# A gated ConvFFN's down projection as seven block products: TensorE work against GpSimd work

## The chip, the core and the metric

The kernel runs on one core of one Trainium2 chip. The metric is the device time of one execution in microseconds (us). Engines are named as in the profile: PE is TensorE, DVE is VectorE, ACT is ScalarE, POOL is GpSimd, SP is SyncE, which only issues transfers here.

## The reference, cut to what matters

The reference is a decoder block: a token mixer, cross-attention to a memory, and a gated feed-forward part (FFN), each followed by a layer norm. Only the FFN and the last norm are touched. `x` is 1024 tokens by 1024 features, `D_FF` is 2816, all float32:

```
u = jnp.einsum('bsd,df->bsf', x, w_up)                  # 1024 -> 2*2816
u = conv_general_dilated(u, conv_w, width 3, causal, per channel) + conv_b
a, g = jnp.split(u, 2, axis=-1)
ff = jnp.einsum('bsf,fd->bsd', silu(g) * a, w_down)     # 2816 -> 1024
x = layer_norm(ALPHA * x + ff, ln3_g, ln3_b)
```

## The kernel before

Every float32 product is made of three passes on TensorE: each operand is split into a rounded high part (a cast on ACT) and the remainder, the low part (one subtraction, on DVE or POOL), and high x high, high x low and low x high are accumulated. So each operand costs one cast and one subtraction each time that it is split.

The FFN has two stages. The **up stage** (`begin`, `end`, `product`) goes through 22 chunks `f` of 128 gated features. Its product is already made in 2x2 blocks by seven block products per chunk (factors A11, A12, S3, S1, S2, A22, S4 of the weight; B11, B21, T3, T1, T2, T4, B22 of the activation); a product is 12 matmuls. For a chunk POOL makes seven low parts and two block sums (`sw`, L1022), DVE makes the other two sums, the convolution (L1098, L1099) and the gating (L1121), and the gated rows of the chunk, `za`, go to a buffer in device memory, `hid`, by a transfer on SP (L1123).

The **down stage** (`load_step`, `fill`, `part`) accumulates over the 22 chunks twice, once for each half of the 1024 output columns. A step is one chunk of one half: the weight rows `w_down` (128x512) and the gated rows `hid` (128x1024) come in, both are cast on ACT, the low part of the weight (`wd`) is made on POOL and that of the rows (`hl`) on DVE, and TensorE runs 8 row tiles x 3 matmuls of 512 columns into 8 PSUM banks. `fill` loads up to `DAHEAD` steps ahead, through three `raw` buffers and through slots of one pool of 47 equal buffers (`Slots`), which are given out in the order in which they were put back. In the last `DROWS` chunks the loop runs row tile by row tile; after each tile DVE adds it to the scaled residual `y`, and in the second half the layer norm of that tile follows: statistics on DVE, two very small operations on POOL (L784, L785), a scaling on ACT and an addition on POOL (L794).

The order of instructions on each engine isn't that of the code: a scheduler orders them by a timeline of its own before the kernel runs, and each engine then takes its queue strictly in that order. A slot's new user waits for its last one.

## Time and profile before

| | |
|---|---|
| median of three runs | 1621.48 us (1620.51 to 1630.96) |
| profiled execution, its own time | 1628.77 us |
| its span, first to last instruction | 1627.1 us |
| mean granted TensorE clock | 0.989 |
| down stage on TensorE, first to last matmul | 1372.94 to 1619.46 us |
| busy in the span: PE / DVE / ACT / POOL | 97% / 60% / 44% / 42% |

Each row of the profile gives a group of instructions or one of them; "idle before" is the time its engine stood still ahead of it, and the arrow names what ended that. Matmuls overlap, so the time that one takes in a stream is read from the starts of neighbours, not from its own duration.

### The profile page before, as it was taken

The numbers are of one execution on the slowest core, as the hardware profiler recorded it, in microseconds if no ns is written. First come the engines' busy times: TensorE is split into PE (matmuls) and PEld (weight loads), VectorE is DVE, ScalarE is ACT, GpSimd is POOL, SyncE is SP. The second block draws the span as 40 slices with busy tenths as digits, with TensorE's granted clock in tenths as the row PEclk, the third lists the DMA queues.
The fourth block names the chain that finished last, engine by engine and source line by source line (L and its number), as shares of the span: only waits on it lengthen the run. The fifth ranks groups of instructions, "written<-read, shape, count | busy, mean of one in ns | idle before, by whom it ended". The sixth has DMA issues, their size and how long they took to land.

```text
span 1627.1 us, 21298 instructions
## 1 busy us (share of the span) xinstructions
PE 1579.6 (97%) x8084; PEld 1336.9 (82%) x8084; DVE 972.0 (60%) x1524; ACT 718.8 (44%) x1235; POOL 688.4 (42%) x540
## 2 busy tenths in 40 slices
PE   8999998999998999999999999999999999999997
PEld 6788887988887988888988878788888888778886
DVE  3856967367577756642456567777666667333325
ACT  4726564156566761133442144454444544442411
POOL 5302222144344741111102657877777773332316
PEclk9999999799999999999999999999999999999999
DMA  6301112132231592311382222222222226663622
GB/s 182 79 1 27 53 52 59 33 91 58 72 107 44 158 281 87 130 40 39 106 264 100 78 65 65 91 78 78 91 81 92 87 71 221 210 203 113 208 61 104
DMA packets 153365, 165.11 MB, mean 101 GB/s; under 512 B 6352, under 2 KB 121112, under 8 KB 153264
## 3 DMA queue, kind: packets, MB, share of 16 engines
q1 hardware_dynamic: 149776, 152.07, 30.4%
q10 hardware_dynamic: 3168, 11.54, 1.9%
q8 instruction: 63, 1.03, 0.3%
q14 instruction: 38, 0.31, 0.1%
q0 software_dynamic: 320, 0.16, 0.0%
HBM read 127.01 MB, written 32.54 MB: 98 GB/s over the span
## 4 chain that ended last, share of the span: by engine, by line
PE 77%; DVE 8%; DMA 6%; ACT 4%; POOL 3%; issue 2%; SPq 0%; POOLq 0%; DVEq 0%; ACTq 0%
PE ps_pj L174 20%; PE ps_S L174 17%; PE ps_t L1078 12%; PE ps_S L1078 6%; PE ps_t L174 5%; PE ps_t L1193 4%; PE ps_S L1193 4%; PE ps_pj L1078 3%; PE ps_pj L1193 2%; DMA raw<-hid 2%; POOL wop L1045 1%; PE ps_t L650 1%; DMA raw<-in_ffn_w_down_dram 1%; PE ps_t L213 1%; DVE p L632 1%
## 5 line engine op out<-in xcount | busy, mean ns | idle before, releaser
L174 PE MATMUL ps_pj<-xT,wh 128*128 128x512 f32 x976 | 313.4, 397 | 0.9 <-DVE KL L593 0.9
L185 POOL TENSOR_TENSOR wl<-raw,wh 128x1024 fp32r<-128x1024 f32 x48 | 120.5, 2511 | 223.5 <-ACT wh L183 213.5
L174 PEld LDWEIGHTS ps_pj<-xT,wh 128*128 128x128 f32 x976 | 180.4, 189 | 34.9 <-DVE KL L593 1.4
L1078 PE MATMUL ps_t<-T,wop 128*128 128x512 f32 x792 | 191.8, 393 | 2.7 <-ACT yg L1107 2.1
L174 PE MATMUL ps_pj<-xT,wl 128*128 128x512 f32 x488 | 192.6, 395 | 0.0
L1078 PEld LDWEIGHTS ps_t<-T,wop 128*128 128x128 f32 x792 | 149.3, 189 | 35.0 <-ACT yg L1107 2.5
L1045 POOL TENSOR_TENSOR wop<-raw,wop 128x512 fp32r<-128x512 f32 x66 | 110.8, 1690 | 86.8 <-ACT wop L1044 86.7
L1045 POOL TENSOR_TENSOR wop<-sw,wop 128x512 fp32r<-128x512 f32 x88 | 134.7, 1553 | 21.8 <-ACT wop L1044 21.8
L1171 POOL TENSOR_TENSOR wd<-raw,wd 128x512 fp32r<-128x512 f32 x44 | 61.0, 1387 | 139.4 <-ACT wd L1170 136.4
L185 DVE TENSOR_TENSOR hl<-raw,hh 128x1024 fp32r<-128x1024 f32 x44 | 54.6, 1242 | 106.1 <-ACT hh L183 106.1
L174 PEld LDWEIGHTS ps_pj<-xT,wl 128*128 128x128 f32 x488 | 91.8, 188 | 17.6
L174 PE MATMUL ps_S<-wh,mh 128*128 128x512 f32 x256 | 100.1, 391 | 0.7 <-ACT mh L183 0.7
L174 PE MATMUL ps_S<-wh,ml 128*128 128x512 f32 x256 | 100.2, 392 | 0.0
L174 PE MATMUL ps_S<-wl,mh 128*128 128x512 f32 x256 | 99.9, 390 | 0.0
L784 POOL TENSOR_SCALAR mv<-mv 128x1 f32<-128x1 f32 x24 | 28.8, 1198 | 159.4 <-DVE mv L783 159.4
L183 ACT CAST wh<-raw 128x1024 fp32r<-128x1024 f32 x64 | 67.2, 1049 | 59.8 <-issue 23.1
L1044 ACT CAST wop<-sw 128x512 fp32r<-128x512 f32 x88 | 54.6, 622 | 86.9 <-POOL sw L1022 58.1
L183 ACT CAST hh<-raw 128x1024 fp32r<-128x1024 f32 x44 | 46.2, 1050 | 90.3 <-DMA raw<-hid 53.7
L1193 PE MATMUL ps_S<-wd,hh 128*128 128x512 f32 x264 | 81.5, 393 | 1.7 <-ACT hh L183 1.7
L1193 PE MATMUL ps_t<-wd,hh 128*128 128x512 f32 x264 | 80.6, 389 | 0.0
L1022 POOL TENSOR_TENSOR sw<-raw 128x512 f32<-128x512 f32 x42 | 66.5, 1582 | 14.6 <-PE ps_t L1078 9.6
L627 POOL TENSOR_TENSOR cdg<-cbc,tri 128x128 f32<-128x128 f32 x64 | 33.0, 518 | 82.0 <-DVE mx L632 61.5
(295 smaller groups left out, 3677.0 us busy)
## 6 DMA issues: line engine op xcount, KB each, us to landing
raw<-in_ffn_w_up_dram SPq DMA_DIRECT2D x44, 512.0 KB, 3.8
raw<-hid SPq DMA_DIRECT2D x44, 512.0 KB, 4.0
raw<-in_w_in_dram SPq DMA_DIRECT2D x24, 512.0 KB, 4.0
hid<-z SPq DMA_DIRECT2D x22, 512.0 KB, 2.6
raw<-in_ffn_w_down_dram SPq DMA_DIRECT2D x44, 256.0 KB, 2.9
raw<-in_xa_wkv_dram SPq DMA_DIRECT2D x16, 512.0 KB, 4.4
x_dram<-y ACTq DMA_DIRECT2D x16, 512.0 KB, 2.6
y<-x_dram SPq DMA_DIRECT2D x16, 512.0 KB, 4.6
```

Source lines behind the costliest of these rows:

```text
L174: nc.tensor.matmul(o, l, r, start=start, stop=stop)
L183: nc.scalar.copy(h, src)
L185: eng.tensor_tensor(l, src, h.bitcast(F32), ALU.subtract)
L213: nc.tensor.transpose(ps[:, k * P:(k + 1) * P], nat[:, kk * P:(kk + 1) * P], ident)
L627: nc.gpsimd.tensor_tensor(cdg, cbc[:, dg], tri, ALU.add)
L784: nc.gpsimd.tensor_scalar(mv[:, 2:3], mv[:, 1:2], LN_EPS, None, ALU.add)
L1022: eng.tensor_tensor(sums[pair][:, i], x0, x1, op)
L1044: nc.scalar.copy(w[:, 0], src)
L1045: nc.gpsimd.tensor_tensor(w[:, 1], src, w[:, 0].bitcast(F32), ALU.subtract)
L1078: nc.tensor.matmul(ps, w[:, part, ws], r, start=first and k == 0 and i == 0, stop=k == 3 and i == 2, skip_group_check=not first)
L1171: nc.gpsimd.tensor_tensor(w[:, 1], raw, w[:, 0].bitcast(F32), ALU.subtract)
L1193: nc.tensor.matmul(banks[st][:, lo:hi], a[:, ss], w[:, r, lo:hi], start=f == 0 and i == 0, stop=f == NF - 1 and i == 2, skip_group_check=l ...
```

## The change

The down projection too is made in 2x2 blocks by seven block products. The blocks are: 512 tokens by 512 tokens, 11 chunks of features by 11 chunks, 512 output columns by 512. For that the chunks are taken in pairs `i` and `11 + i`, also in the up stage. The gated rows are stored as the seven left factors: A11, A12, A22 as they are, S3 = h0 left half minus h0 right half, S1, S2 and S4 as sums and differences of the two chunks of a pair; three of these four are made on POOL and one on DVE at the end of a pair. The seven right factors come from whole rows of `w_down`, which now stay in slots (`wr`); T3, T2 and T4 are made from them by subtractions on POOL, partly in place. A step is one pair `i` of one product `q`: one left factor (128x512) comes in, both factors are cast and split as before, and TensorE runs 4 row tiles x 3 matmuls. `plan` sets the order of the products; each accumulates into one of two groups of four banks, which are added into `y` at the end of each product. Four row tiles are complete after the fifth product and normalized there, the others at the end. `DAHEAD` is 7 and `DROWS` is 7.

```
+    chunks = [c for i in range(HC) for c in (i, HC + i)]
...
+        if f < HC:
+            nc.sync.dma_start(hid_dram[f]["A11"][:, 0], za[:, hs(0)])
+            held[f] = za
+            return
+        to, h0, h1 = hid_dram[f - HC], held.pop(f - HC), za
+        s31, s24 = get([P, 2, 512], name="s31"), get([P, 2, 512], name="s24")
+        nc.sync.dma_start(to["A12A22"], h1.rearrange("p (j s) -> p j s", j=2))
+        nc.gpsimd.tensor_tensor(s31[:, 0], h0[:, hs(0)], h0[:, hs(1)], ALU.subtract)
+        nc.vector.tensor_tensor(s31[:, 1], h0[:, hs(1)], h1[:, hs(1)], ALU.add)
+        nc.sync.dma_start(to["S3S1"], s31)
+        nc.gpsimd.tensor_tensor(s24[:, 0], s31[:, 1], h0[:, hs(0)], ALU.subtract)
+        nc.gpsimd.tensor_tensor(s24[:, 1], h1[:, hs(0)], s24[:, 0], ALU.subtract)
+        nc.sync.dma_start(to["S2S4"], s24)
+        put(h0, h1, s31, s24)
...
+    plan = [("A11", "B11", 0, True), ("S3", "T3", 1, True), ("S2", "T2", 0, False), ("A22", "T4", 1, False),
+            ("S1", "T1", 0, True), ("A12", "B21", 1, True), ("S4", "B22", 0, False)]
+    steps = [(q, i) for q in range(len(plan)) for i in range(HC)]
...
+    def factor(name, i):
+        lo, hi = row(0, i), row(1, i) if name != "B11" else None
+        sub = lambda o, a, b: nc.gpsimd.tensor_tensor(o, a, b, ALU.subtract)
+        if name == "T3":
+            t = small.tile([P, 512], F32, tag="vT", name="t3", bufs=1)
+            sub(t, hi[:, 1], lo[:, 1])
+            return t
+        if name == "T2":
+            sub(lo[:, 1], lo[:, 1], lo[:, 0])
+            sub(lo[:, 0], hi[:, 1], lo[:, 1])
+        if name == "T4":
+            sub(lo[:, 0], hi[:, 0], lo[:, 0])
...
+    def load_step(q, i):
...
+        raw = rawp.tile([P, 512], F32, tag="raw", name="raw")
+        nc.sync.dma_start(raw, hid_dram[i][group][:, j])
+        for src, lo in ((raw, "dve"), (factor(b, i), "pool")):
+            t = get([P, 2, 512], F32R, "dop")
+            split(src, t[:, 0], t[:, 1], lo)
...
+        if b == "T1":
+            put(wrow.pop((0, i)))
...
+            for n, (xp, wp) in enumerate(((0, 0), (0, 1), (1, 0))):
+                nc.tensor.matmul(groups[g][t][:, lo:hi], x[:, xp, ss], w[:, wp, lo:hi],
```

What stands on the engines. On GpSimd, in the down stage before, one row of a step follows the next (`wd`: low part of one chunk's weight):

```order
L1171 TENSOR_TENSOR wd_704_11864<-raw_11862,wd_704_11864 128x512
L1171 TENSOR_TENSOR wd_707_11875<-raw_11873,wd_707_11875 128x512
L1171 TENSOR_TENSOR wd_710_11886<-raw_11884,wd_710_11886 128x512
L1171 TENSOR_TENSOR wd_713_11897<-raw_11895,wd_713_11897 128x512
L1171 TENSOR_TENSOR wd_716_11908<-raw_11906,wd_716_11908 128x512
```

On GpSimd now, where the third product is prepared. A row with L1194 makes a right factor (`wr` for T2 or T4 in place, `t3` for T3), one with L185 a low part; `dop_780` belongs to T3 of pair 10, `dop_796`, `798`, `800` to T2 of pairs 7, 8, 9, and `dop_804` to `810` to T4 of pairs 0 to 3:

```order
L185 TENSOR_TENSOR dop_800_12582<-wr_738_12051,dop_800_12582 128x512
L185 TENSOR_TENSOR dop_780_12358<-t3_12353,dop_780_12358 128x512
L1194 TENSOR_TENSOR wr_735_12029<-wr_772_12303,wr_735_12029 128x512
L185 TENSOR_TENSOR dop_804_12625<-wr_711_11925,dop_804_12625 128x512
L1194 TENSOR_TENSOR wr_729_11985<-wr_766_12255,wr_729_11985 128x512
L1194 TENSOR_TENSOR wr_741_12073<-wr_778_12351,wr_741_12073 128x512
L185 TENSOR_TENSOR dop_806_12646<-wr_714_11935,dop_806_12646 128x512
L1194 TENSOR_TENSOR wr_738_12051<-wr_775_12327,wr_738_12051 128x512
L185 TENSOR_TENSOR dop_808_12667<-wr_717_11945,dop_808_12667 128x512
L185 TENSOR_TENSOR dop_810_12688<-wr_720_11955,dop_810_12688 128x512
L185 TENSOR_TENSOR dop_796_12538<-wr_732_12007,dop_796_12538 128x512
```

The low part of T2's pair 7 now stands behind factors and low parts of the fourth product. From the first `t3` row of the queue to this one there are 72 GpSimd rows, two of them `s24` sums of the last pair, the others L1194 and L185.

On TensorE, in the down stage before, each chunk's matmuls stand in one piece:

```order
L1193 MATMUL ps_S_11821<-wd_710_11886,hh_711_11891 128x512 x2
L1193 MATMUL ps_S_11821<-wd_710_11886,hl_712_11892 128x512
L1193 MATMUL ps_S_11822<-wd_710_11886,hh_711_11891 128x512 x2
L1193 MATMUL ps_S_11822<-wd_710_11886,hl_712_11892 128x512
L1193 MATMUL ps_S_11823<-wd_710_11886,hh_711_11891 128x512 x2
```

On TensorE now, at the same place in the program as GpSimd's rows above (T3 of pair 10, T4 of pairs 0 and 1, T2 of pair 7):

```order
L1240 MATMUL ps_pj_12244<-dop_780_12358,dop_779_12355 128x512 x2
L1240 MATMUL ps_t_12241<-dop_804_12625,dop_803_12622 128x512 x3
L1240 MATMUL ps_t_12241<-dop_806_12646,dop_805_12643 128x512
L1240 MATMUL ps_t_12242<-dop_804_12625,dop_803_12622 128x512 x3
L1240 MATMUL ps_t_12242<-dop_806_12646,dop_805_12643 128x512
L1240 MATMUL ps_S_11911<-dop_796_12538,dop_795_12535 128x512
```

Products are interleaved here. Of the down stage's matmuls 356 stand ahead of the first that reads `dop_796`.

On GpSimd before, layer norms stand only behind all low parts, three rows to a row tile:

```order
L1171 TENSOR_TENSOR wd_821_13077<-raw_13075,wd_821_13077 128x512
L1171 TENSOR_TENSOR wd_824_13112<-raw_13110,wd_824_13112 128x512
L784 TENSOR_SCALAR mv_13219<-mv_13219 128x1
L785 TENSOR_TENSOR mv_13219<-mv_13219,mhalf_115 128x1
L794 TENSOR_TENSOR y_687_11805<-y_687_11805,b_686_11802 128x1024
L784 TENSOR_SCALAR mv_13255<-mv_13255 128x1
```

On GpSimd now, in the sixth product (`dop_875`, `dop_881` are its pairs 8 and 10; `dop_883`, `885` belong to the seventh):

```order
L185 TENSOR_TENSOR dop_881_13373<-wr_778_12351,dop_881_13373 128x512
L784 TENSOR_SCALAR mv_13252<-mv_13252 128x1
L784 TENSOR_SCALAR mv_13264<-mv_13264 128x1
L794 TENSOR_TENSOR y_762_12245<-y_762_12245,b_838_12991 128x1024
L785 TENSOR_TENSOR mv_13252<-mv_13252,mhalf_115 128x1
L785 TENSOR_TENSOR mv_13264<-mv_13264,mhalf_115 128x1
L794 TENSOR_TENSOR y_763_12247<-y_763_12247,b_838_12991 128x1024
L185 TENSOR_TENSOR dop_883_13393<-wr_744_12095,dop_883_13393 128x512
L794 TENSOR_TENSOR y_764_12249<-y_764_12249,b_838_12991 128x1024
L185 TENSOR_TENSOR dop_885_13413<-wr_747_12119,dop_885_13413 128x512
L794 TENSOR_TENSOR y_765_12251<-y_765_12251,b_838_12991 128x1024
L185 TENSOR_TENSOR dop_875_13329<-wr_772_12303,dop_875_13329 128x512
```

Four tiles' norms now stand ahead of low parts that TensorE still needs; before them stand `dop_881` and the first two tiles' small operations.

## Rows read from the trace of the kernel before

**Rows 1.** Busy time of each engine in the whole span (the page).
```profile
PE 1579.6 (97%) x8084; PEld 1336.9 (82%) x8084; DVE 972.0 (60%) x1524; ACT 718.8 (44%) x1235; POOL 688.4 (42%) x540
```

**Rows 2.** Timeline of PE, end of the up stage: start us, us, what.
```profile
1364.78 2.88 PE L1078 MATMUL ps_S<-T,wop 128*128 128x512 f32 x12
1367.50 2.88 PE L1078 MATMUL ps_t<-T,wop 128*128 128x512 f32 x12
1370.22 2.88 PE L1078 MATMUL ps_t<-B,wop 128*128 128x512 f32 x12
1372.94 0.62 PE L1193 MATMUL ps_S<-wd,hh 128*128 128x512 f32 x2
```

**Rows 3.** Windows: PE, PEld, DVE, ACT, POOL busy (x), PEclk, DMA share, GB/s.
```profile
1372.94:1619.46 246.52, 242.49 (x1081) 200.32 (x1079) 92.07 (x95) 81.21 (x94) 86.09 (x63) 0.99 0.48 153
1050.00:1250.00 200.00, 200.00 (x884) 165.62 (x883) 139.02 (x130) 99.83 (x141) 151.11 (x96) 1.00 0.27 85
1452.00:1462.00 10.00, 7.81 (x27) 5.72 (x26) 3.65 (x3) 5.00 (x6) 2.56 (x3) 0.83 0.66 207
```

**Rows 4.** Groups of PE in 1372.94 to 1619.46: the half-width matmuls.
```profile
L1193 PE MATMUL ps_pj<-wd,hh 128*128 128x256 f32 x32 | 5.9, 286 | 0.7 <-DVE y L1209 0.7
L1193 PE MATMUL ps_pj<-wd,hl 128*128 128x256 f32 x16 | 4.5, 282 | 0.0
```

**Rows 5.** Timeline of PE, down stage: idle time in brackets.
```profile
1457.12 0.73 PE L1193 MATMUL ps_S<-wd,hh 128*128 128x512 f32 x2 [1.67 <-ACT hh L183]
```

**Rows 6.** Groups of POOL in 1050 to 1250: busy us, mean ns, idle before.
```profile
L1045 POOL TENSOR_TENSOR wop<-sw,wop 128x512 fp32r<-128x512 f32 x43 | 64.5, 1521 | 8.1 <-ACT wop L1044 8.1
L1045 POOL TENSOR_TENSOR wop<-raw,wop 128x512 fp32r<-128x512 f32 x31 | 54.0, 1756 | 32.4 <-ACT wop L1044 32.4
L1022 POOL TENSOR_TENSOR sw<-raw 128x512 f32<-128x512 f32 x22 | 34.8, 1584 | 5.5 <-PE ps_t L1078 5.3
```

**Rows 7.** Timeline of POOL and DVE, single operations of two collisions.
```profile
1276.28 1.28 POOL L1045 TENSOR_TENSOR wop<-sw,wop 128x512 fp32r<-128x512 f32 x1 [0.73 <-ACT wop L1044]
1277.52 1.76 POOL L1045 TENSOR_TENSOR wop<-sw,wop 128x512 fp32r<-128x512 f32 x1
1279.22 1.74 POOL L1045 TENSOR_TENSOR wop<-sw,wop 128x512 fp32r<-128x512 f32 x1
1276.79 1.33 DVE L1022 TENSOR_TENSOR sw<-raw,sw 128x512 f32<-128x512 f32 x1
...
1270.78 2.27 POOL L1045 TENSOR_TENSOR wop<-raw,wop 128x512 fp32r<-128x512 f32 x1
1273.01 1.28 POOL L1045 TENSOR_TENSOR wop<-sw,wop 128x512 fp32r<-128x512 f32 x1
1270.46 1.44 DVE L1121 TENSOR_TENSOR z<-z,z 128x1024 f32<-128x1024 f32 x1
```

**Rows 8.** Groups of DVE in 1050 to 1250.
```profile
L1113 DVE TENSOR_TENSOR yg<-yg,u 128x512 f32<-128x512 f32 x11 | 16.4, 1494 | 2.6 <-ACT u L1112 2.6
L1022 DVE TENSOR_TENSOR sw<-sw,raw 128x512 f32<-128x512 f32 x11 | 7.6, 693 | 40.4 <-POOL sw L1022 40.4
L1109 DVE TENSOR_TENSOR yg<-yg,ps_t 128x512 f32<-128x512 f32 x11 | 7.5, 680 | 0.0
```

**Rows 9.** Timeline of DVE at the up stage's end: gating of the last two chunks.
```profile
1366.34 1.72 DVE L1121 TENSOR_TENSOR z<-z,z 128x1024 f32<-128x1024 f32 x1
...
1379.27 2.32 DVE L1121 TENSOR_TENSOR z<-z,z 128x1024 f32<-128x1024 f32 x1
```

**Rows 10.** Timeline of POOL at the end of the kernel.
```profile
1609.36 1.19 POOL L784 TENSOR_SCALAR mv<-mv 128x1 f32<-128x1 f32 x1
1610.64 0.56 POOL L785 TENSOR_TENSOR mv<-mv,mhalf 128x1 f32<-128x1 f32 x1
1612.45 2.41 POOL L794 TENSOR_TENSOR y<-y,b 128x1024 f32<-128x1024 f32 x1 [1.26 <-ACT y L793]
1614.83 1.19 POOL L784 TENSOR_SCALAR mv<-mv 128x1 f32<-128x1 f32 x1
...
1620.81 0.78 POOL L784 TENSOR_SCALAR mv<-mv 128x1 f32<-128x1 f32 x1 [0.50 <-DVE mv L783]
```

**Rows 11.** Timeline of SP, one chunk of the up stage.
```profile
1271.93 0.34 SPq L1123 DMA_DIRECT2D hid<-z  x1
1275.57 2.94 SPq L1011 DMA_DIRECT2D raw<-in_ffn_w_up_dram  x2
```

More of the change, by code (lines that the diff above doesn't have):

```diff
@@ L60 @@
 WAHEAD = 6
-DAHEAD = 10
-DROWS = 8
+DAHEAD = 7
+DROWS = 7
 class Slots:
@@ L938, in hybrid_block @@
     rw = lambda ap: ap.rearrange("(c p) -> c p", p=P)
-    hid_dram = [dram.tile([P, S], F32, name=f"hid{f}") for f in range(NF)]
+    HC = NF // 2
+    chunks = [c for i in range(HC) for c in (i, HC + i)]
+    hid_dram = [{name: dram.tile([P, n, 512], F32, name=f"hid{name}{i}")
+                 for name, n in (("A11", 1), ("A12A22", 2), ("S3S1", 2), ("S2S4", 2))} for i in range(HC)]
+    held = {}
     nat, pend, own = {}, [], []
@@ L1061, in hybrid_block @@
                                                       ("S4", "B22")]
-    order = [(f, a) for f in range(LEAD) for a, _ in first]
-    for f in range(NF):
+    order = [(f, a) for f in chunks[:LEAD] for a, _ in first]
+    for n, f in enumerate(chunks):
         order += [(f, a) for a, _ in later]
-        if f + LEAD < NF:
-            order += [(f + LEAD, a) for a, _ in first]
+        if n + LEAD < NF:
+            order += [(chunks[n + LEAD], a) for a, _ in first]
     weights = Weights(order, WAHEAD)
@@ L1143, in hybrid_block @@
     run(ln2)
-    for f in range(LEAD):
+    for f in chunks[:LEAD]:
         begin(f)
-    for f in range(NF):
+    for n, f in enumerate(chunks):
         end(f)
-        if f + LEAD < NF:
-            begin(f + LEAD)
+        if n + LEAD < NF:
+            begin(chunks[n + LEAD])
+            if n + LEAD == NF - 1:
+                for name in ("B11", "B21"):
+                    put(*[t for p in ops.pop(name) for t in p])
     for o in ops.values():
         put(*[t for p in o for t in p])
-    gb = load_gb(ln3_g, ln3_b)
@@ new lines, in hybrid_block, with row @@
+    plan = [("A11", "B11", 0, True), ("S3", "T3", 1, True), ("S2", "T2", 0, False), ("A22", "T4", 1, False),
+            ("S1", "T1", 0, True), ("A12", "B21", 1, True), ("S4", "B22", 0, False)]
+    steps = [(q, i) for q in range(len(plan)) for i in range(HC)]
+    wrow, loaded = {}, {}
+    def row(half, i):
+        if (half, i) not in wrow:
+            wrow[half, i] = get([P, 2, 512], name="wr")
+            r = (half * HC + i) * P
+            nc.sync.dma_start(wrow[half, i].rearrange("p n c -> p (n c)"), w_down[r:r + P, :])
+        return wrow[half, i]
@@ L1214, in hybrid_block @@
                            done=lambda lo, hi: nc.sync.dma_start(out[ss, lo:hi], y[:, lo:hi]))
-        put(*[t for f in range(NF - DROWS, NF) for t in loaded.pop((n, f))])
+                put(y)
 _INS = ['x', 'mem', 'w_in', 'b_fox_f', 'hgrn_lb_logits', 'hgrn_norm_g', 'w_out', 'ln1_g', 'ln1_b',
```

121 lines of the change are left out of this document (71 added, 50 removed).

## The prediction

> **What bounds the kernel now.** I read the page first: PE is busy 97% of the span and no other engine more than 60% [rows 1], so PE's time is the kernel's unless it is made to wait. PE's timeline then gives the price of a matmul: in the up stage 12 matmuls start every 2.72 us, 226.7 ns each, and the down stage starts at 1372.94 [rows 2]. The windows separate the stages [rows 3]. In the last 200 us of the up stage PE is busy all the time, POOL 151.1 us and DVE 139.0 us of 200; in the down stage PE is busy 242.5 of 246.5 us, but POOL only 86.1, DVE 92.1 and ACT 81.2. So GpSimd, the most loaded helper before 1372, has much room after it, and the change fills that room.
>
> The down stage is 2 halves x 22 chunks x 24 = 1056 matmuls of 512 columns; 48 of half width [rows 4] stand for 24 of them. 1056 x 0.2267 = 239.4 us, so 246.5 - 239.4 = 7.1 us are lost: a few waits of the kind of [rows 5], where PE stood 1.67 us for a cast, and stretches such as 1452 to 1462, where the granted clock was 0.83 [rows 3]. With two levels, 1.2 and 2.4 GHz, 0.83 over 10 us is 3.4 us at the lower one and 1.7 us of lost work.
>
> **What the change removes.** Seven products x 11 pairs x 4 tiles x 3 = 924 matmuls remain, 132 fewer: 132 x 0.2267 = **-29.9 us**. The old stage's waits go with it, **-7.1 us**; new ones are priced below.
>
> **What it adds where there is room.** In the up stage three POOL operations and one on DVE per pair. A pair of chunks lasts 2 x 7 x 2.72 = 38.1 us; POOL is busy 151.1/200 x 38.1 = 28.8 us of it, and 3 x 1.597 (the mean of the groups of [rows 6]: 153.3 us for 96) = 4.8 make 33.6. It still fits, with weights prepared six products ahead: I take 0, and 5 us at the upper end, about one pair's addition that comes too late. ACT makes 154 casts of 512 columns where it made 44 of 512 and 44 of 1024, which is 132 of 512: 154/132 x 81.2 = 95 us. DVE makes 77 subtractions of 512 columns, at 0.69 us (the undisturbed price of [rows 8]) 53 us. Both lie beside PE's 209 us (924 x 0.2267) and are hidden. The transfers move about the same bytes (DMA share 0.48 before [rows 3]); a low `w_down` row is loaded again when B21 asks for it after it was put back, 11 rows more. Hidden: 0, and 9 us if the rush of loads around the sixth product doesn't pass at the rates of [rows 3].
>
> **What it adds on GpSimd's path: the third product.** POOL had 44 low parts in this stage. Now it has 77 low parts and 44 factor subtractions (11 for T3, 22 for T2, 11 for T4), 121 in all, and the order puts most of the factors early: T2 and T4 of all pairs stand before PE is half way. The decisive place is the low part of T2's pair 7. It is the 72nd POOL row counted from the first `t3`, and 356 matmuls stand ahead of its reader on PE: 356 x 0.2267 = 80.7 us. POOL is worked out in steps:
>
> Start. The gating of the last chunk but one ends at 1366.34 + 1.72 = 1368.06 [rows 9]; `s31` waits for it, and it and three more rows stand ahead of the first `t3`: 4 x 1.28 = 5.1, so 1373.2, 0.3 us after PE's start of the stage.
>
> Pace. An undisturbed row takes 1276.28 to 1277.52 = 1.24 us; the next one, beside a DVE operation with two SBUF inputs, 1277.52 to 1279.22 = 1.70, so +0.46; beside a 1024-wide one 1270.78 to 1273.01 = 2.23, so +0.99 [rows 7]. 72 x 1.24 = 89.3. In this stretch DVE makes some 31 low parts of rows and sums of 512 columns (+14.3) and four 1024-wide operations (+4.0): 107.6.
>
> A wait. The sixth of the 72 rows, the `s24` sum, needs DVE's sum of the last pair, and the last gating ended at 1381.59 [rows 9]; with 0.69 for the sum it is 1382.3, and POOL is there at 1373.2 + 5 x 1.24 = 1379.4: +2.9.
>
> So `dop_796` is ready at 0.3 + 107.6 + 2.9 = 110.8, and PE has waited 110.8 - 80.7 = **+30.1 us**, in portions, ahead of the third product's and the fourth's matmuls. The row before never shows POOL working through such a queue alone, so the pace is bounded on both sides: no collision, 1.24, gives 92.5 and a wait of 11.8; the up stage's mean with its collisions, 1.597 [rows 6], gives 118.2 and 37.5; every row hit, 1.70, gives 125.6 and 44.9. My 1.49 is between, near the up stage's mean, since DVE's two-input operations are fewer here per POOL row. Behind this place 568 matmuls, 128.8 us of PE, follow, and the low parts they need come by my count at least 6 us early, except for the next place.
>
> The Trainium skill, SBUF — State Buffer, section "Who interferes with whom", says that DVE and GpSimd share one port pair under an exclusive lock, held for a whole instruction, which a DVE operation with two SBUF inputs takes as well. The rows agree on who collides: 1494 ns against 680 ns for the same width with two SBUF inputs and with one [rows 8]. By the lock each short collision would cost a whole 0.69 us (and 1.28 for a long one), not 0.46: 31 x 0.69 + 4 x 1.28 = 26.5 in place of 18.3, and the time would be 8.2 us above mine; nothing below uses that.
>
> After waits of this size I expect PE to run at the lower clock for a stretch as after the wait in [rows 3, 5]: **+1.7 us**, lost work as computed there.
>
> **Layer norms in the sixth product.** Four row tiles are normalized while PE runs the sixth product, and their POOL rows stand ahead of the low part of its pair 8 (`dop_875`). An `mv` pair and an addition cost 1.19 + 0.56 + 2.41 us [rows 10], four tiles 16.6; with three low parts of 1.49, and one wait of 1.26 for ACT's scaling and about 2 us until the first statistics, POOL is there at some 24 us; PE needs it after 8 x 12 = 96 matmuls, 21.8 us. With the pair behind it 1.5 late again: **+3.9 us**, bounds 0 (the norms' chains overlap) and 7 (1.26 for each tile).
>
> **The end.** After the last low parts a tile of the seventh product's last rows is 7 x 3 = 21 matmuls, 4.76 us; before it was 24, 5.44. POOL's chain for a tile is 1.19 + 0.56 + 1.26 + 2.41 = 5.4 us [rows 10] (1609.36 to 1614.83 is 5.47). It was just as fast as PE and is now slower: over the last four tiles the last `mv` comes later by up to 4 x (5.47 - 4.76) = 2.8. Before, it started at 1620.81, 1.35 us after the stage's last matmul [rows 3, 10]; I take **+2.7 us**, bounds 0 and 2.8.
>
> **Sum.** -29.9 - 7.1 + 30.1 + 1.7 + 3.9 + 2.7 = +1.4 us. On the profiled execution's own 1628.77 that is 1630.2; that execution is 7.3 us above the median of 1621.48, so on the median **1622.9 us**. A change of 1%, 16.2 us, is about what a measurement of this kernel can tell from none, so I forecast no measurable difference: the 30 us of matmuls are spent waiting for GpSimd.
>
> **Rivals.** *Faster.* DVE's operations don't hold POOL up, because fewer of them meet a POOL row than I count: 18.3 off the wait, and with quicker norms the 3.9 too, 1622.9 - 18.3 = 1604.6 to 1600.7. If POOL's queue doesn't bind PE at all, only the end remains: 1621.5 - 34.3 = 1587.2. For it speaks that DVE is then only about a third busy; against it that even without collisions 72 rows need 89.3 us and PE gives 80.7, and that POOL lost 0.35 us a row in the up stage beside a DVE at 70%. Chance 0.22.
>
> *Slower.* POOL's own waits for ACT. A low part needs its cast; POOL takes its queue in order, so one late cast holds all factors behind it. 28 of the 72 rows are such low parts. In the up stage a low part waited 8.1/43 = 0.19 us from sums and 32.4/31 = 1.05 us from raw rows [rows 6]; here that is 5 to 29 us more, 1628 to 1652. It decides for slower by over 1% from (16.2 - 1.4)/28 = 0.53 us a row. For it: `t3` has a single buffer, and the low part of T3 needs a cast that can't start until POOL's subtraction ended, a chain POOL -> ACT -> POOL in each pair. Against it: the order puts one or more other rows between the two. Chance 0.20.
>
> *Slower in the up stage.* SyncE issues in order too. The store of S2 and S4 waits for two POOL sums behind the gating, and the next weight loads stand behind it; before, the store went at 1271.93 and the loads behind it at 1275.57 [rows 11], 3.6 us of slack, with more in the six products ahead. Beyond about 6 us each us late costs 11 us over the eleven pairs; two such us make 22, 1645. Chance 0.03.
>
> **Range and chances.** Forecast 0.55. The range, 1597 to 1647, takes in the faster case's upper values and most of the slower case's reach, and leaves out a queue that doesn't bind at all and casts that are late at every low part; the pace's ends (11.8 and 37.5 instead of 30.1) lie within it. Faster 0.22, same 0.55, slower 0.23.
>
> **What would show it.** Right: after 1373 PE runs about 924 full matmuls in some 240 us; PE's largest idle groups are matmuls of L1240 released by POOL L185 in the first 110 us, 25 to 35 us in sum; POOL is busy nine tenths there with a mean near 1.5 us; a second, smaller idle piece stands in the sixth product; the last `mv` comes some 4 us after the last matmul. Up to 1373 nothing moves. Wrong: PE idle released by ACT or by a transfer; a POOL mean of 1.3 (faster) or POOL idle for ACT inside the 72 rows (slower); a later start of the down stage.

## The result

The changed kernel takes 1665.89 us (median; 1664.92 to 1679.85), the kernel before 1621.71 us beside it: a ratio of 1.028 [1.0214, 1.0346] (in brackets, here and below, its 95% interval). It is slower by 44 us; the forecast was 1623, with a range up to 1647.

The page of the kernel after, busy time of each engine in the span (before: [rows 1]):

```profile
PE 1565.8 (94%) x7949; PEld 1314.2 (79%) x7949; DVE 1075.8 (65%) x1588; ACT 730.2 (44%) x1301; POOL 866.0 (52%) x650
```

The same kernel's windows: the up stage, 200 us in its middle, the down stage up to 1518, and the rest of it. Columns as in [rows 3]:

```profile
925.20:1407.70 482.50, 449.04 (x1933) 364.94 (x1932) 350.53 (x300) 209.68 (x310) 362.84 (x232) 0.96 0.30 101
1050.00:1250.00 200.00, 181.92 (x765) 147.70 (x764) 146.43 (x120) 85.75 (x123) 153.96 (x98) 0.96 0.27 88
1407.70:1518.00 110.30, 89.72 (x355) 70.22 (x354) 62.56 (x51) 39.46 (x66) 107.29 (x71) 0.89 0.53 184
1518.00:1656.00 138.00, 131.28 (x589) 108.24 (x587) 82.84 (x97) 53.97 (x87) 99.12 (x70) 0.99 0.42 143
```

The **up stage** is measured from the start of its first matmul to that of its last and takes 1407.6 - 925.2 = 482.4 us; before it took 1372.7 - 935.0 = 437.7. The **down stage** is measured from there to the start of its own last matmul (a few of its matmuls are started earlier, among those of the up stage) and takes 1655.8 - 1407.6 = 248.2 against 246.5. So nearly the whole loss, 44.7 us, lies in the stage of which I had said that nothing moves. (The profiled execution of before began its up stage 9.8 us later than that of after, at 935.0 against 925.2, which is why the stages, and not the spans, are compared.)

In 1050 to 1250 PE was busy 200 of 200 us before and is busy 181.9 now, at a granted clock of 0.96 instead of 1.00, while POOL and DVE do hardly more in the same time: 154.0 and 146.4 us, against 151.1 and 139.0 [rows 3]. No engine's busy share became the bound there; a wait repeats. The up stage of the kernel before, as a whole, to set beside the first window above:

```profile
934.80:1372.94 438.14, 432.66 (x1930) 355.94 (x1929) 300.29 (x289) 210.66 (x302) 311.81 (x198) 1.00 0.28 90
```

PE's idle time grew from 5.5 to 33.5 us, 28 of the lost 44.7; its busy time for the same matmuls grew by 16.4, which goes with the lower granted clock. PE's timeline of the up stage shows the wait once in each pair of chunks (idle time in brackets), nine times from 1068 on:

```profile
1111.29 3.01 PE L1083 MATMUL ps_t<-B,wop 128*128 128x512 f32 x12 [2.31 <-DVE yg L1114]
1153.97 4.53 PE L1083 MATMUL ps_t<-B,wop 128*128 128x512 f32 x12 [3.97 <-DVE yg L1114]
1196.64 4.35 PE L1083 MATMUL ps_t<-B,wop 128*128 128x512 f32 x12 [2.67 <-DVE yg L1114]
```

A pair takes 1196.64 - 1153.97 = 42.7 us instead of 38.1. It is the product S4 x B22, which adds onto the bank that DVE reads in L1114: 2.3 to 4.0 us of waiting, and after it 12 matmuls in 4.4 us instead of 2.88, so that PE ran them for a part at the lower of its two clocks (granted clock 0.64 from 1153.97 to 1158.30).

What makes L1114 late is followed back through three engines. The timelines of POOL, ACT and DVE, in this order and one fence each, from the end of a pair to the next chunk's read:

```profile
1163.85 5.86 POOL L1050 TENSOR_TENSOR wop<-raw,wop 128x512 fp32r<-128x512 f32 x3 [2.82 <-ACT wop L1049]
1169.67 1.29 POOL L1138 TENSOR_TENSOR s<-s,z 128x512 f32<-128x512 f32 x1
1171.04 1.29 POOL L1139 TENSOR_TENSOR s<-z,s 128x512 f32<-128x512 f32 x1
1172.29 2.54 POOL L1027 TENSOR_TENSOR sw<-raw 128x512 f32<-128x512 f32 x2
...
1182.85 1.89 POOL L1027 TENSOR_TENSOR sw<-raw 128x512 f32<-128x512 f32 x1 [0.34 <-DMA raw<-in_ffn_w_up_dram]
1187.56 4.16 POOL L1050 TENSOR_TENSOR wop<-raw,wop 128x512 fp32r<-128x512 f32 x2 [2.82 <-ACT wop L1049]
1191.68 1.29 POOL L1050 TENSOR_TENSOR wop<-sw,wop 128x512 fp32r<-128x512 f32 x1
1192.93 1.28 POOL L1027 TENSOR_TENSOR sw<-raw 128x512 f32<-128x512 f32 x1
1194.17 1.26 POOL L1135 TENSOR_TENSOR s<-z 128x512 f32<-128x512 f32 x1
```

```profile
1173.61 0.62 ACT L1049 CAST wop<-sw 128x512 fp32r<-128x512 f32 x1 [5.60 <-POOL sw L1027]
1174.13 0.58 ACT L1117 COPY u<-ps_S 128x512 f32<-128x512 f32 x1
...
1185.91 1.06 ACT L1122 ACTIVATE z<-z 128x1024 f32<-128x1024 f32 x1 [3.14 <-DVE z L1104]
1186.87 1.12 ACT L1049 CAST wop<-raw 128x512 fp32r<-128x512 f32 x2
```

```profile
1174.75 0.69 DVE L1118 TENSOR_TENSOR yg<-yg,u 128x512 f32<-128x512 f32 x1 [4.46 <-ACT u L1117]
1175.36 1.78 DVE L1027 TENSOR_TENSOR sw<-sw,raw 128x512 f32<-128x512 f32 x1
...
1181.19 2.39 DVE L1103 SCALAR_TENSOR_TENSOR z<-yg,cw,z 128x1023 f32<-128x1023 f32 x1 [1.16 <-ACT z L1102]
1183.62 2.20 DVE L1104 SCALAR_TENSOR_TENSOR z<-yg,cw,z 128x1022 f32<-128x1022 f32 x1
...
1194.24 1.74 DVE L1027 TENSOR_TENSOR sw<-sw,raw 128x512 f32<-128x512 f32 x1 [3.67 <-POOL sw L1027]
1195.91 0.68 DVE L1114 TENSOR_TENSOR yg<-yg,ps_t 128x512 f32<-128x512 f32 x1
```

POOL makes the weight's sums `sw` (1172.29) behind three low parts and the two `s24` sums. ACT's cast of `sw` waits 5.60 us for them, and the copy of `u` stands behind it. DVE waits 4.46 us for `u`; its sums and convolution behind that come late and run beside POOL (2.39 and 2.20 us for the convolution's first half, 1.27 and 1.28 for the second). ACT's silu waits for the convolution (3.14), the casts stand behind the silu, POOL's low parts behind the casts (2.82), the next `sw` behind those, and DVE's own `sw` waits 3.67 for it, with L1114 right behind. It is a loop through four queues, each taken strictly in order.

The same read in the kernel before, where it is L1109, from the timelines of DVE and of PE:

```profile
1142.30 0.69 DVE L1022 TENSOR_TENSOR sw<-sw,raw 128x512 f32<-128x512 f32 x1 [3.68 <-POOL sw L1022]
1142.91 0.68 DVE L1109 TENSOR_TENSOR yg<-yg,ps_t 128x512 f32<-128x512 f32 x1
```

```profile
1147.18 2.88 PE L1078 MATMUL ps_t<-B,wop 128*128 128x512 f32 x12
```

DVE waited 3.68 us for POOL's `sw` there too, and the read ended at 1143.59 (1142.91 + 0.68), 3.6 us ahead of the product that needs its bank. So the chain of waits is not new: at this read it had 3.6 us to spare, and a lateness below that could not be seen on PE.

### The profile page after: what moved, and what is told of

It reads as the page before. It is cut to its first block, busy times and chain, and to the rows that moved or that the text cites. A ratio compares the mean times of both kernels' runs of the same rounds, so it can differ in the third digit from the quotient of the medians.

```text
span 1664.0 us, 21417 instructions
## 1 busy us (share of the span) xinstructions
PE 1565.8 (94%) x7949; PEld 1314.2 (79%) x7949; DVE 1075.8 (65%) x1588; ACT 730.2 (44%) x1301; POOL 866.0 (52%) x650
## 4 chain that ended last, share of the span: by engine, by line
PE 54%; POOL 16%; DVE 12%; issue 7%; ACT 6%; DMA 4%; SPq 0%; POOLq 0%; DVEq 0%; ACTq 0%
PE ps_pj L174 20%; PE ps_S L174 16%; POOL wop L1050 6%; PE ps_t L174 4%; PE ps_S L1240 3%; POOL wr L1194 3%; PE ps_t L1083 3%; DVE sw L1027 2%; PE ps_t L1240 2%; POOL sw L1027 2%; DVE z L1103 2%; PE ps_S L1083 2%; DVE z L1104 1%; POOL dop L185 1%; ACT wop L1049 1%
## 5 line engine op out<-in xcount | busy, mean ns | idle before, releaser
L185 POOL TENSOR_TENSOR wl<-raw,wh 128x1024 fp32r<-128x1024 f32 x48 | 118.0, 2459 | 217.8 <-ACT wh L183 207.9
L1050 POOL TENSOR_TENSOR wop<-sw,wop 128x512 fp32r<-128x512 f32 x88 | 141.6, 1627 | 36.0 <-ACT wop L1049 36.0
L1050 POOL TENSOR_TENSOR wop<-raw,wop 128x512 fp32r<-128x512 f32 x66 | 118.0, 1804 | 76.6 <-ACT wop L1049 76.6
L185 DVE TENSOR_TENSOR dop<-raw,dop 128x512 fp32r<-128x512 f32 x77 | 93.3, 1226 | 87.2 <-ACT dop L183 86.6
L1240 PE MATMUL ps_S<-dop,dop 128*128 128x512 f32 x396 | 102.3, 403 | 16.9 <-POOL dop L185 9.7
L185 POOL TENSOR_TENSOR dop<-wr,dop 128x512 fp32r<-128x512 f32 x66 | 97.9, 1499 | 26.0 <-ACT dop L183 26.0
L1240 PEld LDWEIGHTS ps_S<-dop,dop 128*128 128x128 f32 x396 | 76.7, 195 | 35.8 <-POOL dop L185 11.7
L1240 PE MATMUL ps_t<-dop,dop 128*128 128x512 f32 (+1 forms) x351 | 92.1, 390 | 10.4 <-POOL dop L185 5.0
L1083 PE MATMUL ps_t<-B,wop 128*128 128x512 f32 x264 | 77.8, 449 | 25.1 <-DVE yg L1114 25.1
L183 ACT CAST wh<-raw 128x1024 fp32r<-128x1024 f32 x64 | 67.2, 1050 | 59.9 <-issue 23.6
L1083 PEld LDWEIGHTS ps_t<-B,wop 128*128 128x128 f32 x264 | 56.6, 218 | 41.5 <-DVE yg L1114 29.1
```

The costliest lines, as they stand in the source:

```text
L183: nc.scalar.copy(h, src)
L185: eng.tensor_tensor(l, src, h.bitcast(F32), ALU.subtract)
L1050: nc.gpsimd.tensor_tensor(w[:, 1], src, w[:, 0].bitcast(F32), ALU.subtract)
L1083: nc.tensor.matmul(ps, w[:, part, ws], r, start=first and k == 0 and i == 0, stop=k == 3 and i == 2, skip_group_check=not first)
L1240: nc.tensor.matmul(groups[g][t][:, lo:hi], x[:, xp, ss], w[:, wp, lo:hi], start=first and i == 0 and n == 0, stop=i == HC - 1 and n == 2, ...
```

## The experiments

Stage times below are taken as above, in one profiled execution of each; kernel times are medians, and ratios are those of all runs to the kernel before. Executions of one kernel lie up to 20 us apart (1632.98 to 1652.92 in the run with one slot less), so a stage time from one of them has an uncertainty that isn't known: the down stage of the changed kernel, with no edit to it, took 243.3 to 254.7 us in these executions.

**Four kernels on the first theory**, that the sums of the pair in POOL's queue are the cause. All four sums on DVE:

```
-        nc.gpsimd.tensor_tensor(s31[:, 0], h0[:, hs(0)], h0[:, hs(1)], ALU.subtract)
+        nc.vector.tensor_tensor(s31[:, 0], h0[:, hs(0)], h0[:, hs(1)], ALU.subtract)
...
-        nc.gpsimd.tensor_tensor(s24[:, 0], s31[:, 1], h0[:, hs(0)], ALU.subtract)
+        nc.vector.tensor_tensor(s24[:, 0], s31[:, 1], h0[:, hs(0)], ALU.subtract)
```

> All four sums of a pair in the up stage on DVE, none on POOL. Theory (the up stage's 44 us come from the three POOL sums that stand ahead of the weights' sums sw in POOL's queue, so that ACT's copy of u and DVE's PSUM reads behind them come late): up stage back to 438 to 445 us, kernel 1622 to 1630. Rival (DVE is as tight: its queue then holds 2.6 to 5 us of sums ahead of the PSUM read): up stage stays at 470 to 490, kernel 1655 to 1675. Rival (pair order and the stores of the pairs): no change, 1666.

Up stage 473.4, kernel 1658.32, 1.0208 [1.0159, 1.0258]. Only 9 of 45 us come back: the first rival. The sums left out:

```
-        s31, s24 = get([P, 2, 512], name="s31"), get([P, 2, 512], name="s24")
...
+        nc.sync.dma_start(to["S3S1"], h0.rearrange("p (j s) -> p j s", j=2))
+        nc.sync.dma_start(to["S2S4"], h1.rearrange("p (j s) -> p j s", j=2))
+        put(h0, h1)
```

> The four sums of a pair are left out: the gated rows themselves are stored in their places by transfers of the same size, so the factors S3, S1, S2, S4 of the down projection hold other data; pair order, stores and the whole down stage stay. Theory (the sums): up stage 438 to 442, kernel 1620 to 1625, with the down stage's 248 us unchanged. Rival (pair order, rows held longer, stores on SyncE ahead of the weight loads): up stage stays at 475 to 485, kernel 1658 to 1668.

Up stage 466.6, kernel 1648.85, 1.0146 [1.0102, 1.0190]. Between the two: without a single sum 29 of the 45 us are still there. So the sums account for 16 us here. The sums written out one chunk later:

```
         product(f, "S4", "B22", pd, False)
         nc.vector.tensor_tensor(ya[:, hs(1)], u, pd, ALU.add)
+        if late:
+            sums()
```

> The same sums on the same engines, but written out one chunk later, so that in POOL's queue they stand behind the weights' sums sw of the next chunk instead of ahead of them. Theory (place in the queue): up stage 438 to 455, kernel 1622 to 1640. Rival (amount: POOL at 76% with its collisions can't do three more operations in the loop POOL, DVE, PE wherever they stand): up stage 470 to 485, kernel 1655 to 1668.

Up stage 481.4, kernel 1674.60, 1.0317 [1.0259, 1.0375]: the theory of the place in POOL's queue falls. Most of PE's wait moved to another read, ACT's copy of `yg`. The factors of the down stage on DVE:

```
-        sub = lambda o, a, b: nc.gpsimd.tensor_tensor(o, a, b, ALU.subtract)
+        sub = lambda o, a, b: nc.vector.tensor_tensor(o, a, b, ALU.subtract)
```

> The 44 factor subtractions of the down stage on DVE instead of POOL; the up stage as it was. Theory (in the down stage PE waits for POOL's queue, 30 us in the first 110): the 72 POOL rows become 40, the waits fall to 0 to 8 us, kernel 1636 to 1644. Rival (the waits come from ACT's casts, 22.8 us by the page's releasers, and casts have to wait for the factors wherever they are made): 1655 to 1666.

Down stage 237.3 instead of 248.2, kernel 1662.17, 1.0215 [1.0152, 1.0278]; the kernel's time is the rival's, and the down stage gave back 11 us, not 22 to 30. POOL's rows are a part of that wait; PE now waited 6.92 and 6.05 us for casts whose factor DVE makes behind the last convolution.

**Three kernels on what is left without sums.** The pair order alone:

```
-        if f < HC:
-            nc.sync.dma_start(hid_dram[f]["A11"][:, 0], za[:, hs(0)])
-            held[f] = za
...
+        nc.sync.dma_start(hid_dram[f % HC]["S3S1" if f < HC else "A12A22"], za.rearrange("p (j s) -> p j s", j=2))
+        put(za)
```

> The up stage of the kernel before, but for the order of the chunks (i, 11 + i): each chunk's gated rows are stored whole as soon as they are made and their slot is given back at once; no sums, nothing held. The down stage is that of the changed kernel, fed from these two tensors, so its left factors hold other data. Theory now (the 29 us that are left of the up stage's 44 when the sums are left out come from the rows that are held for a chunk and from the larger stores, through the slots and through the queue order that follows from them): up stage 437 to 441, kernel 1620 to 1625. Rival (the order of the chunks, or the early loads of the down stage): up stage 460 or more, kernel 1643 or more.

Up stage 438.1, kernel 1619.58, 0.9988 [0.9963, 1.0013]. The up stage is as the theory had it. Its windows (up stage, its middle, down stage):

```profile
925.50:1363.90 438.40, 432.89 (x1931) 356.04 (x1930) 301.79 (x291) 213.88 (x310) 318.06 (x202) 1.00 0.29 94
1050.00:1250.00 200.00, 200.00 (x884) 165.62 (x883) 136.41 (x128) 98.27 (x140) 151.21 (x96) 1.00 0.27 84
1363.90:1607.20 243.30, 221.29 (x945) 177.90 (x943) 144.56 (x147) 93.24 (x153) 199.07 (x136) 0.96 0.46 158
```

PE is busy 200 of 200 us again. And this is the new down stage behind an up stage that is left alone: 243.3 us. Then the same with the first rows' slot held to the pair's end:

```
+        if f < HC:
+            held[f] = za
+        else:
+            put(held.pop(f - HC), za)
-        put(za)
```

> As the run before, but the slot of a pair's first rows is held until the pair's end; the same two stores, no sums. Its order on DVE differs from the order without the hold: in every second chunk one of the weights' sums stands ahead of the convolution and the other ahead of the PSUM read. Theory (the held slot alone changes the queues' order, and this makes the PSUM reads late): up stage 455 to 467, kernel 1638 to 1650. Rival (the third and fourth store of a pair, behind which weight loads and slots wait): up stage 437 to 442, kernel 1620 to 1626.

Up stage 451.7, kernel 1649.32, 1.0165 [1.0123, 1.0206]: 14 us in the up stage for a slot that is given back a chunk later, with no instruction or byte more; a little less than the theory's range. The profiled execution is the fastest of the five here, by 9.5 us, and by the medians the kernel lost 30 us against the pair order alone (1619.58). The changed kernel with the weights' casts and sums behind the PSUM reads:

```
+        def refill(self, read):
+            with tc.issue_after(read.ins):
+                while self.todo and len(self.ready) < self.ahead:
+                    self.load()
...
-        nc.scalar.copy(u, pa)
+        weights.refill(nc.scalar.copy(u, pa))
```

> The changed kernel with all its sums, held rows and stores, but the casts and sums of the weights stand behind the PSUM read of the product during which they were written out, on that read's engine (ACT or DVE), and a product's slot is given back before the next is taken. Theory (PE waits because ACT's and DVE's PSUM reads stand in their queues behind casts and sums that wait for POOL, and not because POOL has too much work): up stage 438 to 455, kernel 1622 to 1639. Rival (amount: with 76% busy and its collisions POOL can't make the low parts and three sums in 38.1 us a pair): up stage 470 to 485, with PE waiting for the products' weights instead, kernel 1655 to 1668.

Up stage 460.2, kernel 1651.21, 1.0167 [1.0122, 1.0213]: 22 of 45 us come back, between theory and rival. Its window in the middle of the up stage:

```profile
1050.00:1250.00 200.00, 194.58 (x847) 159.36 (x846) 160.88 (x126) 89.29 (x130) 182.00 (x105) 0.99 0.30 98
```

POOL is at 182 of 200 us: with the reads out of the way it is nearly full, at 1.73 us an operation instead of 1.57 (182.00/105 and 153.96/98), so a part of its busy time is lengthening beside DVE.

**One slot less, and the read's slack.** The pair order alone, with one slot taken out of use:

```
+    spare = get([P, S], name="spare")
+    nc.gpsimd.memset(spare[:, 0:1], 0.0)
     for f in chunks[:LEAD]:
         begin(f)
...
+    put(spare)
```

> The run with the pair order alone, with one slot of the pool of 47 taken out of use during the up stage and nothing held besides. On DVE the PSUM read now stands ahead of both sums of the weights in each chunk. Theory (one slot less is enough, because casts and sums then wait for slots): up stage 448 to 456 as in the run that holds rows, kernel 1630 to 1640. Rival (what counts is the order that the queues took: here the PSUM read stands first): up stage 437 to 442, kernel 1618 to 1624.

Up stage 451.1, kernel 1643.70, 1.0125 [1.0069, 1.0180]: one slot of 47 is worth 13 us of the up stage (24 us of the kernel by the medians), though on DVE the read stands first here. DVE's read L1114 now waited for ACT's copy of `yg`, 36.1 us in sum between 940 and 1360. The product S4 later:

```
         end(f)
         if n + LEAD < NF:
             begin(chunks[n + LEAD])
...
+        end2(f)
```

> The changed kernel, but in the up stage the product S4 x B22 of a chunk, which adds onto the bank that DVE's late read frees, is made after the next chunk's two A products: that read has 5.4 us more. Theory (PE loses its 44 us at this one read, which is 3 to 4 us late per pair beyond a slack of 3.6): up stage 438 to 450, kernel 1621 to 1634. Rival (the loop through POOL, ACT and DVE can't turn faster than 42.7 us a pair, wherever PE waits): up stage 475 to 485, kernel 1658 to 1668, with PE waiting at another read or at weights.

Up stage 480.8, kernel 1670.93, 1.0296 [1.0265, 1.0327]: the rival. L1114 no longer holds PE up; ACT's copy of `yg` and the weights do. T2 on DVE:

```
-            sub(lo[:, 1], lo[:, 1], lo[:, 0])
-            sub(lo[:, 0], hi[:, 1], lo[:, 1])
+            nc.vector.tensor_tensor(lo[:, 1], lo[:, 1], lo[:, 0], ALU.subtract)
+            nc.vector.tensor_tensor(lo[:, 0], hi[:, 1], lo[:, 1], ALU.subtract)
```

> The 22 subtractions of the factor T2 in the down stage on DVE, T3 and T4 still on POOL; up stage untouched. Theory (the down stage's first 110 us wait for POOL's queue): POOL's 72 rows become about 50, the down stage falls from 248 to 226 to 234 us, kernel 1644 to 1652. Rival (as with all 44 on DVE, where 11 us came back: casts wait for the factors anyway, and DVE is late with them beside the last convolution): 235 to 240 us, kernel 1653 to 1659.

Down stage 239.8, kernel 1658.87, 1.0223 [1.0189, 1.0258]: 8 us, the rival's numbers. Both together, the two diffs above in one kernel:

> Both of the last two edits in one kernel. If both theories hold, up stage 438 to 450 and down stage 226 to 234, kernel 1599 to 1618, below the kernel before; if only one holds, 1640 to 1655; if neither, 1655 to 1668.

Up stage 482.1, down stage 243.5, kernel 1662.29, 1.0253 [1.0206, 1.0301]: the up stage gains nothing and the down stage 5 us.

**Slots or order?** S2 and S4 written over the pair's first rows:

```
-        s31, s24 = get([P, 2, 512], name="s31"), get([P, 2, 512], name="s24")
+        s31, s24 = get([P, 2, 512], name="s31"), h0.rearrange("p (j s) -> p j s", j=2)
```

> In the up stage S2 and S4 are written over the pair's first rows, so that the slot s24 isn't taken: one slot more, same work on each engine. Theory (slots): the up stage loses about 13 us of its 44, 465 to 472, kernel 1649 to 1656. Rival (amount of work in the loop): 480 to 484, kernel 1663 to 1668.

Up stage 482.6, kernel 1666.63, 1.0274 [1.0238, 1.0309]: nothing. Weights four products ahead:

```
-WAHEAD = 6
+WAHEAD = 4
```

> The up stage prepares its weights four products ahead instead of six: two slots more are free, same work on each engine. Theory (slots): up stage 438 to 460, kernel 1622 to 1643. Rival (amount of work, or weights that come late for want of lookahead): 480 or more, kernel 1664 or more, with PE waiting for weights.

Up stage 459.4, kernel 1649.49, 1.0166 [1.0133, 1.0200]: 23 us, the theory's upper end in the up stage, while the kernel is above its range. Reads first without its edges (the orders to the scheduler that keep an instruction behind a read in its queue):

```
-            with tc.issue_after(read.ins):
-                while self.todo and len(self.ready) < self.ahead:
-                    self.load()
+            while self.todo and len(self.ready) < self.ahead:
+                self.load()
```

> As the run with reads first (up stage 461), but without its edges in the queues: only the slot of a product is given back before the next is taken. Theory (slots): up stage 455 to 468, kernel 1645 to 1655, as with the edges. Rival (the order in the queues was what helped there): 475 to 484, kernel 1658 to 1667.

Up stage 496.7, kernel 1682.76, 1.0374 [1.0336, 1.0412]: outside both. Against 460.2 with the edges, the same work with the same slots differs by 36 us (32 by the kernels' medians) through the order in ACT's and DVE's queues. All three together (reads first with edges, in place, `WAHEAD = 5`):

> Reads first with its edges, S2 and S4 over the pair's first rows, and weights five products ahead: together some three slots more than in the changed kernel. Theory (slots): up stage 438 to 446, kernel 1621 to 1631. Rival (amount of work): not below the 461 us of reads first alone, kernel 1643 or more.

Up stage 482.6, kernel 1672.92, 1.0305 [1.0264, 1.0346]: in the rival's range; with more slots and the reads first PE now waits for the weights' casts and low parts. Edges alone:

```
+            with ExitStack() as behind:
+                for r in reads.values():
+                    behind.enter_context(tc.issue_after(r))
...
-        nc.scalar.copy(u, pa)
+        read("act", nc.scalar.copy(u, pa))
```

> The changed kernel with edges alone: each cast and sum of the weights stands behind the last PSUM reads written out before it, on ACT and on DVE; slots are taken and given back as in the changed kernel. Theory (order in the queues: a PSUM read behind a cast or a sum that waits is what makes PE wait): up stage 445 to 465, kernel 1629 to 1650. Rival (slots, or the amount of work): 478 or more, kernel 1662 or more.

Up stage 472.1, kernel 1658.07, 1.0222 [1.0195, 1.0248]: 10 us, between. The same with `WAHEAD = 4`:

> The same edges with weights four products ahead instead of six (23 us less in the up stage without edges). Theory (order): with the reads first at every place and two slots more, up stage 438 to 455, kernel 1621 to 1640. Rival (too little lookahead once the reads go first: PE waits for weights, as in the run with three slots more): 475 or more, kernel 1658 or more.

Up stage 481.4, kernel 1669.28, 1.0303 [1.0263, 1.0343]: the rival's time, but not its reason: between 940 and 1360 PE waited 20.5 us for ACT's copy of `yg` and some 6 for weights. The edges took back what four products ahead had given.

**The change without touching the up stage.** Rows stored whole at once; the sums of the left factors made in the down stage, on DVE:

```
+        if a == "S3":
+            nc.sync.dma_start(raw, h["h0"])
+            sub(raw[:, 0], raw[:, 0], raw[:, 1])
+        if a == "S2":
...
+            sub(both[:, 0], raw[:, 1], both[:, 1], ALU.add)
+            sub(both[:, 1], both[:, 0], raw[:, 0])
+            nc.sync.dma_start(h["S1S2"], both)
```

> Up stage as in the run with the pair order alone: gated rows stored whole, nothing held. The 44 sums of the left factors are made in the down stage on DVE, when a step needs them (S3 in the second product, S1 and S2 in the third, where they are stored, S4 in the last); the factors of the weight stay on POOL. Theory (the sums cost 44 us only where a loop of queues has 3 us of slack; DVE has 70 idle us in the first 110 of the down stage): up stage 438, down stage 245 to 258, kernel 1619 to 1634. Rival (44 more two-input operations on DVE beside POOL's 72 rows, and a third and fourth row in flight through three buffers, delay POOL and the casts by as much): down stage 270 or more, kernel 1645 or more.

Up stage 439.7, down stage 269.4, kernel 1642.81, 1.0124 [1.0097, 1.0151]. The up stage is as the theory had it, the down stage nearly as the rival had it: 26 us more than behind the pair order alone. The smallest loss of the complete kernels tried, and still slower than before. PE's waits in it are many and small (23 of up to 3.6 us), most released by ACT's casts:

```profile
1386.32 1.46 PE L1252 MATMUL ps_S<-dop,dop 128*128 128x512 f32 x3 [3.58 <-ACT dop L183]
1475.40 1.65 PE L1252 MATMUL ps_S<-dop,dop 128*128 128x512 f32 x3 [2.80 <-ACT dop L183]
1489.91 2.50 PE L1252 MATMUL ps_S<-dop,dop 128*128 128x512 f32 x5 [2.96 <-DVE dop L185]
```

## Why the prediction was wrong

**The step that failed** is the one on where there is room: "POOL is busy 151.1/200 x 38.1 = 28.8 us of it, and 3 x 1.597 ... = 4.8 make 33.6. It still fits, with weights prepared six products ahead: I take 0, and 5 us at the upper end". It cost 44.7. The sum of busy times was nearly right (POOL 153.96/200 x 42.7 = 32.9 us a pair), but it doesn't say whether the work fits: PE at 200 of 200 us in [rows 3] hid that the queues beside it were only just in time. One path through the experiments adds the pieces, each with the last one's: pair order 438.1, a held slot 451.7 (+13.6), the larger and more stores 466.6 (+14.9), the sums 482.4 (+15.8). Two of the three pieces put no operation on an engine, and together they are more than half of it. How the 28.5 us of these two divide isn't settled: by the kernels' medians the same path goes 1619.58, 1649.32, 1648.85 and 1665.89, so that the held slot costs 30, the stores nothing and the sums 17. I had priced neither piece: the prediction doesn't mention that `h0` keeps its slot for a chunk, and the new stores only as a rival on SyncE's queue, at a chance of 0.03. That rival named the stage and the "each us late costs 11"; whether it also named the place differs from kernel to kernel. In the changed kernel the raw load was late by 0.34 us at POOL in the loop shown above (1182.85). On the way there loads and stores were waited for. What POOL and ACT waited for between 940 and 1360 in the run without sums (us in sum, times, longest):

```profile
POOL sw L1027 <- DMA raw<-in_ffn_w_up_dram: 32.1, 10, 4.7
ACT wop L1049 <- DMA hidS2S<-z: 26.2, 9, 3.1
```

The first wait is 30.8 us in the run that holds rows, 5.2 with the pair order alone and 8.4 in the changed kernel. The second line is a cast that stands until a store has landed: a slot's new user waits for its last one, which here is the store, so more stores can cost time through the slots too. In the changed kernel that wait is down to 2.9 us, and the waits that count are for casts, sums and reads.

The other error in that step is that I counted what collisions cost POOL and not what they cost DVE. The groups of DVE in 1050 to 1250 of the kernel after (before: [rows 8]):

```profile
L1104 DVE SCALAR_TENSOR_TENSOR z<-yg,cw,z 128x1022 f32<-128x1022 f32 x10 | 19.9, 1985 | 0.2
L1103 DVE SCALAR_TENSOR_TENSOR z<-yg,cw,z 128x1023 f32<-128x1023 f32 x10 | 18.4, 1838 | 12.4 <-ACT z L1102 12.4
L1027 DVE TENSOR_TENSOR sw<-sw,raw 128x512 f32<-128x512 f32 x9 | 15.8, 1758 | 18.3 <-POOL sw L1027 18.3
```

`sw<-sw,raw` took 693 ns before [rows 8] and 1758 now: POOL is at work when its turn comes (1194.24 in the loop above stands beside POOL's operation at 1194.17).

**The down stage's time came out, in part by luck.** Forecast: the matmuls, the old waits, POOL's queue, the clock and the norms give -29.9 - 7.1 + 30.1 + 1.7 + 3.9 = -1.3 us. Measured +1.7 behind the disturbed up stage and 243.3 - 246.5 = -3.2 behind an undisturbed one. That PE loses some 30 us early in the stage, beside a POOL that is hardly ever idle (107.3 of 110.3 us busy), held; the place and the start didn't. The rows of POOL from the last `t3` row on, and PE's rows beside them:

```profile
1510.64 1.71 POOL L185 TENSOR_TENSOR dop<-t,dop 128x512 fp32r<-128x512 f32 x1
1512.31 1.29 POOL L1194 TENSOR_TENSOR wr<-wr,wr 128x512 f32<-128x512 f32 x1
1513.57 1.28 POOL L185 TENSOR_TENSOR dop<-wr,dop 128x512 fp32r<-128x512 f32 x1
1514.81 3.54 POOL L1194 TENSOR_TENSOR wr<-wr,wr 128x512 f32<-128x512 f32 x2
1518.32 1.27 POOL L185 TENSOR_TENSOR dop<-wr,dop 128x512 fp32r<-128x512 f32 x1
1519.55 1.28 POOL L1194 TENSOR_TENSOR wr<-wr,wr 128x512 f32<-128x512 f32 x1
1520.80 5.02 POOL L185 TENSOR_TENSOR dop<-wr,dop 128x512 fp32r<-128x512 f32 x4
```

```profile
1517.80 0.85 PE L1240 MATMUL ps_S<-dop,dop 128*128 128x512 f32 x3
1519.64 1.65 PE L1240 MATMUL ps_t<-dop,dop 128*128 128x512 f32 x6 [0.76 <-POOL dop L185]
1527.93 1.52 PE L1240 MATMUL ps_S<-dop,dop 128*128 128x512 f32 x6
```

In the queue's order `dop_806` (the fourth product's pair 1) is the row at 1518.32, the 68th of the 72, and PE waits for it at 1519.64. `dop_796`, the decisive place of the forecast, is the third of the four at 1520.80 and ready at 1524.6, 117.0 us after the stage's start (forecast 110.8). PE didn't wait for it: the first matmuls of that step, with 356 of the stage's ahead of them, went at 1517.80, before POOL had made the low part, so they read the high parts alone; by their count and banks the others of the step, with 396 ahead, begin at 1527.93. I had taken the first reader of the tile for the reader of its low part. With row 68 and the 360 matmuls ahead of its reader my own figures give 0.3 + 2.9 + 68 x 1.49 - 360 x 0.2267 = 22.9, not 30.1. What made up for it is the start: POOL began the rows at 1414.95, not 0.3 but 7.3 us into the stage. Its pace was nearly as forecast, (1524.57 - 1414.95)/72 = 1.52 us a row (forecast 1.49), and no wait of POOL's for ACT shows among them, so the first slower rival didn't occur.

The losses also lay earlier than I had them, "ahead of the third product's and the fourth's matmuls". The window of the first product, and PE's two longest waits in it:

```profile
1407.70:1459.13 51.43, 34.91 (x128) 26.68 (x126) 32.47 (x23) 17.47 (x28) 48.58 (x32) 0.80 0.72 260
```

```profile
1430.85 2.93 PE L1240 MATMUL ps_S<-dop,dop 128*128 128x512 f32 x6 [6.66 <-POOL dop L185]
1444.47 1.65 PE L1240 MATMUL ps_S<-dop,dop 128*128 128x512 f32 x3 [4.88 <-ACT dop L183]
```

Some 125 matmuls, 28.3 us of work (125 x 0.2267), took 51.4: 23 us of loss. Over the first 110.3 us of the stage PE did 356 matmuls' worth, 80.7 us, so 29.6 were lost (forecast 30.1 and 1.7). But of these 110.3 - 89.7 = 20.6 us are idle, 12 of them ended by POOL and 8.5 by ACT's casts, and 89.7 - 80.7 = 9.0 went to longer matmuls, with the clock at 0.89 in this window: the term of 1.7 was too small, the one of the waits too large. That POOL alone makes this wait isn't so: with 44 factors taken off it only 11 us came back, with T2 alone 8, and PE then waited for casts.

**Norms and end.** The norms in the sixth product cost two waits of 1.83 us, 3.7 (forecast 3.9); which rows stood ahead was as the order showed. From the last matmul's start on the end cost nothing: 8.2 us to the last instruction against 7.9 (forecast +2.7). But just ahead of that, PE waited 2.29 us for DVE's addition of the last tile's first half and then ran the second half at the lower clock, 3.91 us instead of 2.67: some 3.5 us that I hadn't priced, and the reason why POOL's chain of 5.46 us a tile could keep up.

**What stays open.** Which wait closes the loop of the up stage isn't settled, nor how the loss divides between the held slot and the stores. Shown: the three pieces together make it (438.1 without them), and it is not the sums' place in POOL's queue (481.4), not the slack of one read (480.8), and not slots alone (giving one back by writing in place 482.6, two by less lookahead 459.4). Order alone moved the same work by 36 us one way (496.7 to 460.2) and edges on top of less lookahead by 22 the other way (459.4 to 481.4). In the two best kernels with the sums (460.2 and 459.4) POOL is 91% and 90% busy in 1050 to 1250, so a part of the last 22 us may be plain amount; that wasn't separated.
